# S5 tables formed unit by unit, with the chunk-state inputs taken from on-chip S tables inside the v projection slots

## The chip, the cores and the metric

One core of a Trainium2 chip runs the program. The metric is device time in microseconds (us) for one launch, as a median over runs. Engines are written as in the profile: PE is TensorE, PEld its weight loads, DVE VectorE, ACT ScalarE, POOL GpSimd, SP SyncE; SPq and ACTq are those engines' work of issuing DMAs. Matmul operands are split into a high and a low part (float32r), so a product of two matrices is three passes.

## The reference, cut to what matters

One layer works on 128 context tokens and 512 latent tokens (NT = 640). The part in question is the mixer: a chunked gating half (u, v) and a state-space half ("S5": 64 groups of 16 channels, one 64-dim complex state for each group and direction).

```
def ssm_discretize(lam_re, lam_im, log_dt, b_re, b_im):
    lam_bar = jnp.exp(lam * dt)
    b_bar = ((lam_bar - 1.0) / lam)[..., None] * b
    return lam_bar, b_bar
def ssm_scan(u, lam_bar, b_bar, h0, reverse):
    bu = jnp.einsum("gph,blgh->blgp", b_bar, u)
    _, h = lax.associative_scan(_scan_combine, (a, bu), axis=1, reverse=reverse)
def s5_mixer(...):
    y = (jnp.einsum("ghp,blgp->blgh", c_f, h_f) + jnp.einsum("ghp,blgp->blgh", c_b, h_b)).real
    y = gelu(y + d_skip * x);  y = y * sigmoid(y @ w_glu + b_glu)
def trunk_layer(...):
    u_a, v_a, u_b = jnp.split(h @ p["w_in"], [D_CHUNK, 2 * D_CHUNK], axis=-1)
    y_a = chunk_mlp_mixer(u_a, v_a, ...)      # per chunk of 128: u * (w_s @ rmsnorm(v) + b_s)
    y_b, hf, hb = s5_mixer(u_b, ...)
    mix = concatenate([rmsnorm(y_a), rmsnorm(y_b)]) @ p["w_out"]
```

## The kernel before

**Order of the work.** First the modulation and the first norm (h_chunk) run beside the projection of the S5 input (u_chunk); that order is set by a scheduler that works on the program as written. From line 433 on each instruction is kept in program order (all of these show line L445 in the profile), and a hand-written plan of slots sets it: `slot` (line 490) runs the phases sp, evac, act, dve, pe, end, and `at(t, phase, f)` puts a piece of work into slot t. Most slots hold one weight chunk: its load is issued two slots ahead (`raw_of`), its split into high (ACT, `hi_of`) and low part (DVE, `lo_of`, tile `wl`) one slot ahead, and its matmuls run in the slot. Chunks 0 to 15 are the v projection (slots 0 to 15; tile `ws`), 16 to 31 the u projection (slots 16 to 31), 32 to 47 half of the output projection (slots 33 to 48; tile `as`; slot 32 has no chunk), 48 to 55 the GLU. Elementwise work that belongs to no slot comes from a generator, `flow[0]`: `run_flow` takes operations from it until their noted cost reaches a number. In slots 0 to 15 it is `tables`, later `scan`.

**The S5 half by chunks of 8 positions.** The 640 positions give NJ = 81 columns of 8 (one is a zero). The S5 input goes from `u_chunk` to DRAM as `ud` (channel, position in the chunk, column), one store for each of 8 channel blocks, from the tile `us`. `tables` first multiplies the whole of b by the discretisation factor (24 DVE operations of 512 elements on `btab`), then builds, for each of 16 units of 4 groups (`unit`), the table St (chunk input to state, 6 DVE operations of 512 elements, transposed on PE as `sp`, evacuated as SS, stored to DRAM as `sd`), the table O (state to output, 6 operations of 576, stored as `od`) and the convolution kernel (`kp`, `ks`, stored as `kd`). After slot 16, `tables_done` closes that pool, loads the S5 input again as `U` (16 loads of 16 partitions, pieces of 81 elements) and the `sd` tables as `st_`; `s5_in` (line 784; four units in each of slots 17 to 20) multiplies them (tile `x1p`) into the scan's array X. From slot 21 `scan` runs on DVE in the flow. The slot after it ends is called e; from there `s5_rest` puts two units of `s5_out` (tile `yp`) into each slot, stores the result to DRAM (`yd`), loads it back by channel (`yc`), applies gelu, and after slot e + 10 the GLU follows. `ada_step` puts pieces of the modulation of the later layers (1 MB of weights, four matmuls `adaq`) into slots that the loop at line 1113 names.

**Tiles and names of the rows.** `us`, `vo` and other short-lived tiles share the tag t25 with two buffers; PSUM tiles named `sp`, `x1p`, `vtp`, `z`, `yp` share the tag px with two; `vc` is the v projection loaded back for the chunk mixer, transposed as `vtp`. `so` holds what `s5_out` loads (`od` by SP, `kd` by ACT). `aw` is a piece of modulation weights, `wr` a raw weight chunk.

Of the kernel before, what the change touches and what calls it, by code (L numbers as in the profile page):

```python
# [43 lines left out]
def build(nc, tc, a, out, tap=None):  # L44
# [254 lines left out]
    def u_chunk(kc0, nk):  # L299
        kb = slice(kc0, kc0 + nk)  # L300
        cpl = 8 // nk
        for cb in range(8):
# [12 lines left out]
            else:  # L315
# [6 lines left out]
                nc.gpsimd.dma_start(ud[cb * 128:(cb + 1) * 128], us)  # L322
# [8 lines left out]
    ctab, btab = [big[:, 2 * NT_ + t * 4096:2 * NT_ + (t + 1) * 4096].rearrange("p (i c) -> p i c", i=2) for t in range(2)]  # L331
# [251 lines left out]
    yad = dram("yad", [128, NT])  # L583
# [53 lines left out]
    SY.dma_start(ctab[:, 0, :], a["c1"])  # L637
# [8 lines left out]
    def ch(tab, i, d, g0, n):  # L646
        return mkap(tab, i * 2048 + (d * NG + g0) * GH, [[GH, 4], [0, n], [1, GH]])

    def tables():


        S.activation(btab[:, 1, :], btab[:, 1, :], AF.Copy, scale=nsgn)
        g3 = lambda t: t.rearrange("p (g h) -> p g h", h=GH)
        e_b = lambda t, s: t[:, s:s + 32].unsqueeze(2).broadcast_to([128, 32, GH])
        for s in range(0, 128, 32):
            b1, b2 = g3(btab[:, 0, s * GH:(s + 32) * GH]), g3(btab[:, 1, s * GH:(s + 32) * GH])
            u1 = g_.tile([128, 32, GH], F32, name="u1", tag="go", bufs=8)
            u2 = g_.tile([128, 32, GH], F32, name="u2", tag="go", bufs=8)
            V.tensor_tensor(u1, b2, e_b(ei, s), op=OP.mult)
            yield 0.7  # L660
            V.tensor_tensor(u2, b1, e_b(ei, s), op=OP.mult)
            yield 0.7
            V.tensor_tensor(b1, b1, e_b(er, s), op=OP.mult)
            yield 0.7
# [12 lines left out]
    kps = {}

    def unit(u):
        g0 = u * 4  # L680
        St = g_.tile([128, 2, 4, 8, GH], F32, name="St", tag="gs", bufs=4)
        for d in range(2):
            s0, st = (0, 1) if d == 0 else (7, -1)
            t2 = g_.tile([128, 4, 8, GH], F32, name="t3", tag="gt2", bufs=2)
# [16 lines left out]
        at(now[0] + 1, "pe", s_mm)
        if u == 0:
            V.tensor_scalar(ctab[:, 1, :], ctab[:, 1, :], -1.0, None, op0=OP.mult)
            yield 1.3
        O = [g_.tile([128, 4, 9, GH], F32, name="O", tag="go", bufs=8) for _ in range(2)]
# [43 lines left out]
        at(n + 1, "pe", k_copy)  # L749

# [12 lines left out]
    udv = ud.rearrange("(g c) t j -> t c g j", c=GH)  # L763
    ydv = yd.rearrange("(g c) t j -> t c g j", c=GH)
# [5 lines left out]
    Us, pbs, st_ = [], {}, {}  # L770
    X = None

    def u_load(half):
        U = pbs["uy"].tile([128, HG, NJ], F32, name="U", tag="uy", bufs=2)
        Us.append(U)
        for tq in range(8):
            SY.dma_start(U[(7 - tq) * GH:(8 - tq) * GH], udv[tq][:, half * HG:(half + 1) * HG, :])

    def st_load(u):
        if u < 16:  # L780
            st_[u] = pbs["pb"].tile([128, 2, 4, 128], F32, name="st_", tag="so", bufs=3)
            SY.dma_start(st_[u].rearrange("p d g c -> p (d g c)"), sd[u])

    def s5_in(u):

        for d in range(2):
            p = px("x1p")
            for g in range(4):
                gg = 4 * u + g
                T.matmul(p[:, g * NJ:(g + 1) * NJ], st_[u][:, d, g, :], Us[gg // HG][:, gg % HG, :], start=True, stop=True)  # L790
            pv = p[:, 0:4 * NJ].rearrange("p (g j) -> p g j", j=NJ)
# [933 lines left out]
```

## Time and profile before

| what | value |
|---|---|
| median of 3 runs | 2790.15 us (2788.37 to 2792.84) |
| the profiled execution's own time | 2791.73 us |
| its span | 2789.9 us |
| PE busy, of the span | 2625.2 us (94%) |
| DVE busy | 1942.8 us (70%) |
| ACT busy | 1102.2 us (40%) |
| mean granted TensorE clock | 0.962 of full speed |
| HBM traffic over the span | 190 GB/s |

The profile page has one execution. Busy shares are means over stages with different limits: the second half of the span (the MLP) has PE at 90% or more in nearly every slice, while the stage of this change, from some 235 us to 866 us, has slices with PE in the 60s and 70s of per cent and DVE anywhere from 10 to 90%. The rows below are from there. Slot numbers are put to times by counting the groups of `ws` and `as` matmuls.

### The profile page before, as it was taken

How to read it: one execution, taken by the hardware profiler on the slowest of the kernel's cores; microseconds unless marked ns; L12 is line 12 of the kernel's file. 1: busy time of each engine (PE TensorE's matmuls, PEld its weight loads, DVE VectorE, ACT ScalarE, POOL GpSimd, SP SyncE). 2: the span in 40 equal slices, each digit the busy share in tenths (PEclk: the TensorE clock that was granted, in tenths of full speed). 3: DMA queues.
4: the chain of work that ended last, by engine and by line, in shares of the span. 5: the costliest groups of instructions: out<-in, count | busy, mean ns of one | idle time of the engine just before them, and what ended most of it. 6: DMA issues, size and time to landing. Idle time of an engine off the chain costs nothing.

```text
span 2789.9 us, 42919 instructions
## 1 busy us (share of the span) xinstructions
PE 2625.2 (94%) x17217; PEld 2428.4 (87%) x17217; DVE 1942.8 (70%) x2839; ACT 1102.2 (40%) x1757; POOL 73.3 (3%) x89
## 2 busy tenths in 40 slices
PE   8998888999976997799999999999899999999997
PEld 5687778977765765799999999999899999999996
DVE  4567991689615455777777777777667777777786
ACT  4121321222213335655555555555433322333253
POOL 0000220000000000000000000000000000000000
PEclk9999998999967999899999999999999999999998
DMA  9846679554575686255555555556565355446453
GB/s 297 290 166 232 210 230 209 154 183 140 170 213 149 243 297 253 72 170 178 181 181 183 176 176 177 183 181 220 195 223 194 105 215 215 146 168 222 160 186 112
DMA packets 464231, 534.12 MB, mean 191 GB/s; under 512 B 34672, under 2 KB 377616, under 8 KB 456352
## 3 DMA queue, kind: packets, MB, share of 16 engines
q1 hardware_dynamic: 450288, 522.62, 57.9%
q10 hardware_dynamic: 13104, 6.10, 1.0%
q8 instruction: 136, 2.23, 0.3%
q0 software_dynamic: 640, 2.65, 0.3%
q14 instruction: 63, 0.52, 0.1%
HBM read 416.14 MB, written 115.16 MB: 190 GB/s over the span
## 4 chain that ended last, share of the span: by engine, by line
PE 78%; DVE 9%; DMA 7%; ACT 2%; issue 2%; SPq 1%; ACTq 0%; POOL 0%; DVEq 0%; POOLq 0%
PE X L1348 32%; PE Y L1348 16%; PE Z L1348 8%; PE ws L445 5%; PE ub L186 4%; PE as L445 4%; PE ob L1251 3%; PE ada L196 2%; DVE t L445 1%; DVE O L445 1%; DMA wr<-in_w_out_dram 1%; DVE St L445 1%; PE x1p L445 1%; DMA x2d<-wx 1%; PE adaq L445 1%
## 5 line engine op out<-in xcount | busy, mean ns | idle before, releaser
L1335 ACT ACTIVATE wh<-wx 128x1024 fp32r<-128x1024 f32 x223 | 235.9, 1058 | 310.5 <-PE X L1348 144.6
L1340 DVE TENSOR_TENSOR wl<-wx,wh 128x1024 fp32r<-128x1024 f32 x223 | 272.8, 1223 | 73.9 <-ACT wh L1335 71.9
L1348 PE MATMUL X<-B,wh 128*128 128x320 f32 x1376 | 306.1, 310 | 3.0 <-ACT wx L1335 3.0
L1348 PEld LDWEIGHTS X<-B,wh 128*128 128x128 f32 x1376 | 232.0, 189 | 3.2 <-ACT wx L1335 3.2
L1348 PE MATMUL X<-B,wl 128*128 128x320 f32 x688 | 213.2, 310 | 0.0
L1348 PE MATMUL Y<-B,wh 128*128 128x320 f32 x672 | 150.9, 313 | 4.7 <-ACT wh L1335 4.7
L1348 PE MATMUL X<-B,wx 128*128 128x320 f32 x1008 | 154.6, 309 | 0.0
L1348 PEld LDWEIGHTS X<-B,wx 128*128 128x128 f32 x1008 | 149.5, 188 | 0.0
L1423 DVE TENSOR_TENSOR wx<-wx 128x320 fp32r<-128x320 f32 x192 | 93.0, 485 | 77.9 <-ACT wx L1420 77.9
L1546 DVE TENSOR_TENSOR facc<-facc,X 128x640 f32<-128x640 f32 x116 | 95.1, 820 | 74.4 <-PE X L1348 73.7
L445 PE MATMUL ws<-hTh,wl 128*128 128x320 f32 x512 | 123.2, 323 | 21.0 <-DVE wl L445 21.0
L445 ACT ACTIVATE wh<-wr 128x1024 fp32r<-128x1024 f32 x56 | 59.4, 1060 | 192.5 <-DMA wr<-in_w_in_dram 58.1
L1348 PE MATMUL X<-B2n,wh 128*128 128x320 f32 x608 | 134.7, 309 | 0.0
L1348 PEld LDWEIGHTS X<-B,wl 128*128 128x128 f32 x688 | 130.1, 189 | 0.0
L445 PE MATMUL ws<-hTh,wh 128*128 128x320 f32 x512 | 125.0, 326 | 1.2 <-DVE us L321 1.2
L1335 ACT ACTIVATE wh<-wr 128x1024 fp32r<-128x1024 f32 x76 | 80.4, 1058 | 110.6 <-PE X L1348 51.5
L445 PE MATMUL ws<-hTl,wh 128*128 128x320 f32 x512 | 121.3, 319 | 0.0
L1335 ACT ACTIVATE wx<-wr 128x1024 fp32r<-128x1024 f32 x75 | 79.3, 1058 | 104.5 <-PE X L1348 49.0
L1335 ACT ACTIVATE wx<-wx 128x1024 fp32r<-128x1024 f32 x74 | 78.3, 1058 | 103.7 <-PE X L1348 48.4
L1348 PEld LDWEIGHTS Y<-B,wh 128*128 128x128 f32 x672 | 114.2, 191 | 4.9 <-ACT wh L1335 4.9
L1340 DVE TENSOR_TENSOR wx<-wr,wx 128x1024 fp32r<-128x1024 f32 x75 | 91.8, 1224 | 28.4 <-ACT wx L1335 27.6
L445 PEld LDWEIGHTS ws<-hTh,wl 128*128 128x128 f32 x512 | 90.0, 198 | 23.6 <-DVE wl L445 23.5
(411 smaller groups left out, 6651.8 us busy)
## 6 DMA issues: line engine op xcount, KB each, us to landing
wx<-in_w_ff_dram SPq DMA_DIRECT2D x169, 512.0 KB
x2d<-wx SPq DMA_DIRECT2D x224, 320.0 KB
wr<-in_w_ff_dram SPq DMA_DIRECT2D x87, 512.0 KB
aw<-in_w_ada_dram SPq DMA_DIRECT2D x80, 512.0 KB
was<-in_w_ada_dram SPq DMA_DIRECT2D x64, 512.0 KB
B2n<-x2d SPq DMA_DIRECT2D x24, 1280.0 KB
wr<-in_w_in_dram SPq DMA_DIRECT2D x48, 512.0 KB
wr<-in_w_out_dram SPq DMA_DIRECT2D x48, 512.0 KB
```

The lines of the kernel that those rows point to most:

```text
L186: T.matmul(p[:, :n], st[:, kk, c:c + 128], mv(k)[:, t0:t0 + n], start=(first and i == 0), stop=(last and i == 2))
L196: T.matmul(p[32 * j:32 * j + 32], sc[:, 2 * (k0 + i):2 * (k0 + i) + 32], w[:, i, :], start=k0 + i < 4, stop=k0 + i >= NK - 4)
L445: return lambda *p, **k: P(f(*p, **k))
L1251: T.matmul(p, st[:, k0 + kk, tsl], mv[:, kk, :], start=(k0 + kk == 0 and i == 0), stop=(k0 + kk == 7 and i == 2))
L1335: P(S.activation(hls[n][0], raw, AF.Copy))
L1340: P(V.tensor_sub(lo, raw, hi.bitcast(F32)))
L1348: P(T.matmul(p, st[:, j, c:c + 128], xv(j, x), start=first and j == 0 and i == 0, stop=j == nj - 1 and i == 2, skip_group_check=not first))
L1423: P(V.tensor_sub(hlt[i][:, 1], raw, hlt[i][:, 0].bitcast(F32)))
L1546: P(V.tensor_add(dst, dst, src))
```

## The change

In words, in the order of the program:

- `ud` becomes (partition = 16 x (7 - position in the chunk) + channel in the group, group, column). Each `us` is stored by 8 DMAs of 128 pieces of 81 elements (324 bytes) where one DMA of 128 pieces of 648 elements stood; for the first six channel blocks four of the eight are issued by ACT, the rest by POOL.
- b and c come as one array `bc`, 512 columns (256 KB) for each unit, three buffers, instead of four arrays of 1 MB. The powers of lambda and the factors er, ei are copied by ACT from `big` to `tabs`, and X takes the memory of `big` from then on.
- The 24 operations of 512 on all of b become 6 operations of 128 elements in each of 16 units. St has 2 buffers where it had 4, O 4 where it had 8.
- SS is not stored. `s5_in(u - 1)` runs in slots 2 to 16, in `s_mm(u)` ahead of the transposes of unit u, on SS and on `xin`, a load of 4 groups of `ud` (162 KB); ACT writes both directions into X, where ACT and DVE wrote one each.
- `sd`, `st_` and 16 loads of U go; U is loaded whole, in two DMAs of 128 partitions of 10 KB, after slot 16. The detour of ya through DRAM (`yad`) goes.
- `scan` starts in slot 17 (before: 21), `ada_step` is also called in slots 17 to 20, 36 and 40, and no longer from slot e to slot 48.

The core of the diff:

```diff
-                nc.gpsimd.dma_start(ud[cb * 128:(cb + 1) * 128], us)
+                for t in range(L):
+                    (nc.scalar if t % 2 and cb < 6 else nc.gpsimd).dma_start(
+                        bass.AP(tensor=ud.tensor, offset=ud.offset + ((7 - t) * GH * NG + cb * 8) * NJ,
+                                ap=[[NJ, 8], [NG * NJ, GH], [1, NJ]]), us[:, t, :])
...
+    tabs = g_.tile([128, 2 * NT_ + 256], F32, name="tabs")
+    bcs, xin = {}, {}
+    def bc_load(u):
+        if u < 16:
+            bcs[u] = g_.tile([128, 4, 2, 4, GH], F32, name="bc", tag="bc", bufs=3)
+            SY.dma_start(bcs[u].rearrange("p t d g h -> p (t d g h)"), a["bc"][:, u * 512:(u + 1) * 512])
+    bc_load(0)
     raw_of(0)
-    for i, nm in enumerate(("b1", "b2")):
-        SY.dma_start(btab[:, i, :], a[nm])
+    S.activation(tabs[:, 0:2 * NT_], big[:, 0:2 * NT_], AF.Copy)
+    S.activation(tabs[:, 2 * NT_:], big[:, 3712 + 9 * 128:3712 + 11 * 128], AF.Copy)
...
     raw_of(1)
+    bc_load(1)
+    bc_load(2)
     hi_of(0)
     lo_of(0)
+    X = a40([128, 2, NG, NJ + 1], F32, "X")
...
+    def u_unit(u):
+        xin[u] = g_.tile([128, 4, NJ], F32, name="xin", tag="xin", bufs=2)
+        SY.dma_start(xin[u], ud[:, 4 * u:4 * u + 4, :])
     def tables():
...
+        for u in range(16):
+            b1, b2, c1 = [bcs[u][:, t] for t in range(3)]
+            S.activation(b2, b2, AF.Copy, scale=nsgn)
+            S.activation(c1, c1, AF.Copy, scale=sgn)
+            e_b = lambda t: mkap(t, u * 4, [[NG, 2], [1, 4], [0, GH]])
...
+            V.tensor_tensor(u1, b2, e_b(ei), op=OP.mult)
+            V.tensor_tensor(u2, b1, e_b(ei), op=OP.mult)
+            yield 0.5
+            V.tensor_tensor(b1, b1, e_b(er), op=OP.mult)
+            V.tensor_tensor(b2, b2, e_b(er), op=OP.mult)
+            yield 0.5
             V.tensor_add(b1, b1, u1)
...
+    def s5_in(u):
+        SS, U = sss.pop(u), xin.pop(u)
+        for d in range(2):
+            p = px("x1p")
+            for g in range(4):
+                T.matmul(p[:, g * NJ:(g + 1) * NJ], SS[d][:, g * 128:(g + 1) * 128], U[:, g, :], start=True, stop=True)
+            S.activation(X[:, d, 4 * u:4 * u + 4, (1 - d):(1 - d) + NJ], p[:, 0:4 * NJ].rearrange("p (g j) -> p g j", j=NJ), AF.Copy)
...
         def s_mm():
-            SS = g_.tile([128, 2, 512], F32, name="SS", tag="gss", bufs=2)
+            if u:
+                s5_in(u - 1)
...
-            SY.dma_start(sd[u], SS.rearrange("p d c -> p (d c)"))
+        at(now[0] + 1, "sp", lambda: u_unit(u))
         at(now[0] + 1, "pe", s_mm)
...
+        at(n + 1, "pe", lambda: bc_load(u + 3))
...
-    for u in range(16):
-        at(17 + u // 4, "pe", lambda u=u: s5_in(u))
+    at(16, "pe", lambda: s5_in(15))
+    at(16, "end", lambda: tables_done())
...
-        if t == 21:
+        if t == 17:
             flow[0] = scan()
...
-        if scanned and e is None:
+        if scanned and e is None and t >= 38:
...
-            if 21 <= t < 32 or t > 34 and t % 4:
+            if 17 <= t < 32 or t > 34 and e is None:
                 ada_step(t)
-            slot(True, *((0, 0) if t < 21 else (2.0, 4.6) if t < 32 else (0.0, 2.0) if t == 33 else (2.0, 5.0)))
+            slot(True, *((0, 0) if t < 17 else (2.0, 4.6) if t < 32 else (0.0, 2.0) if t == 33 else (2.0, 5.0)))
```

**Where instructions move.** First ACT at the end of the S5 input projection, before: the splits of weight chunks (`wh`; L175 is `load_w`, L445 the slots), then the first table work.

```order
L256 ACTIVATE hTh_899<-tp,AS 128x128
L175 ACTIVATE wh<-wr 128x1024 x2
L445 ACTIVATE wh<-wr 128x1024 x2
L445 ACTIVATE big<-big,nsgn 128x2048
L445 ACTIVATE wh<-wr 128x1024
L445 ACTIVATE big<-big,sgn 128x2048
```

The same place on ACT in the change (L174 is `load_w`, L323 the stores of `us`, L447 the slots).

```order
L255 ACTIVATE hTh_898<-tp,AS 128x128
L174 ACTIVATE wh<-wr 128x1024
L323 DMA ud<-us 8x16x81 x8
L174 ACTIVATE wh<-wr 128x1024
L323 DMA ud<-us 8x16x81 x16
L447 ACTIVATE tabs<-big 128x2304
L447 ACTIVATE tabs<-big 128x256
L447 ACTIVATE wh<-wr 128x1024 x2
```

Twenty-four DMA issues and the two copies to `tabs` now stand ahead of the high parts of chunks 0 and 1; on POOL 40 issues stand where 8 stood.

Next PE in a v slot before, from the last matmuls of a chunk to the first of the next chunk.

```order
L445 MATMUL ws_3323<-hTh_224,wl 128x320
L445 MATMUL kp<-O,big 32x128 x8
L445 MATMUL sp<-ident,St 128x128 x8
L445 MATMUL kp<-O,big 32x128 x8
L445 MATMUL adaq<-aw,sc 32x512 x4
L445 MATMUL ws_3322<-hTh_899,wh 128x320
```

And PE in a v slot of the change.

```order
L447 MATMUL ws_2704<-hTh_223,wl 128x320
L447 MATMUL x1p<-xin,SS 128x81 x8
L447 MATMUL sp<-ident,St 128x128 x8
L447 MATMUL kp<-O,bc 32x128 x8
L447 MATMUL adaq<-aw,sc 32x512 x4
L447 MATMUL ws_2703<-hTh_898,wh 128x320
```

Each of 15 transposes of a unit in the v slots now has the 8 matmuls `x1p` of the unit before ahead of it; the 32 in each of slots 17 to 20 are gone, and unit 15's stand in slot 16.

Last SP where slot 16 passes into slot 17, before.

```order
L445 DMA wr<-in_w_in_dram 128x8x128
L445 DMA U<-ud 16x32x81 x8
L445 DMA st__4011<-sd 128x1024
L445 DMA st__4013<-sd 128x1024
L445 DMA st__4015<-sd 128x1024
L445 DMA U<-ud 16x32x81 x8
L445 DMA wst<-in_w_s_dram 128x128
L445 DMA bsb<-in_b_s_dram 128x128
L445 DMA vc<-vd 128x640
```

And the same place on SP in the change.

```order
L447 DMA wr<-in_w_in_dram 128x8x128
L447 DMA U<-ud 128x2592 x2
L447 DMA wst<-in_w_s_dram 128x128
L447 DMA bsb<-in_b_s_dram 128x128
L447 DMA vc<-vd 128x640
L447 DMA vd<-vo 128x640
```

Two large loads of U stand ahead of `vc` where 16 small ones and three of `st_` stood, and nothing in slots 17 to 20 loads a table. Further on, the first `yp` matmuls stand behind the 15th of the 16 `as` chunks before, and behind the 11th in the change: e is slot 47 before and slot 43 in the change.

## Rows read from the trace of the kernel before

**Rows 1.** Windows: length, busy (count) PE, PEld, DVE, ACT, POOL; clock, DMA, GB/s.

```profile
235.05:425.30 190.25, 166.40 (x1246) 148.48 (x1247) 174.16 (x240) 53.90 (x120) 42.02 (x58) 0.92 0.72 226
433.80:464.90 31.10, 22.10 (x119) 21.55 (x119) 5.51 (x20) 2.71 (x5) 0.00 (x0) 0.65 1.09 210
464.90:511.60 46.70, 46.55 (x363) 46.31 (x363) 11.06 (x19) 11.56 (x26) 0.00 (x0) 0.98 0.54 164
511.60:617.30 105.70, 99.67 (x700) 89.78 (x698) 90.75 (x216) 22.44 (x48) 9.42 (x5) 1.00 0.53 164
617.30:706.50 89.20, 83.47 (x377) 62.73 (x377) 83.61 (x195) 26.18 (x34) 3.19 (x2) 0.96 0.47 157
706.50:737.90 31.40, 31.40 (x146) 22.82 (x145) 29.93 (x73) 7.80 (x10) 0.00 (x0) 1.00 0.39 134
737.90:866.00 128.10, 88.40 (x529) 70.22 (x525) 27.93 (x51) 26.73 (x45) 0.00 (x0) 0.72 0.77 207
```

**Rows 2.** Timeline of PE in a v slot: start, us, operation, idle before.

```profile
353.66 0.67 PE L445 MATMUL kp<-O,big 128*32 128x128 f32 x16
...
354.26 1.09 PE L445 MATMUL sp<-ident,St 128*128 128x128 f32 x8
...
355.28 1.07 PE L445 MATMUL adaq<-aw,sc 128*32 128x512 f32 x8
...
358.97 0.56 PE L445 MATMUL ws<-hTh,wl 128*128 128x320 f32 x2 [1.82 <-DVE wl L445]
```

**Rows 3.** Groups by shape, 235 to 440 us: busy us, mean ns, idle before.

```profile
L445 DVE TENSOR_TENSOR St<-big 128x512 f32<-128x512 f32 x32 | 22.0, 688 | 0.0
...
L445 DVE TENSOR_TENSOR big<-big,u 128x512 f32<-128x512 f32 x8 | 5.5, 690 | 0.2
```

**Rows 4.** Waits, 235 to 440 us: total us, times, longest.

```profile
PE ws L445 <- DVE wl L445: 21.0, 9, 3.4
...
DVE big L445 <- DMA big<-in_c_dram: 4.4, 1, 4.4
```

**Rows 5.** Chain that ended last, 425 to 475 us: start, us, what.

```profile
433.93 7.79 DMA U<-ud
...
446.61 7.19 DMA U<-ud
...
453.87 6.51 DMA st__4180<-sd
```

**Rows 6.** Timeline of PE in slot 18: first and last of four units.

```profile
472.97 1.91 PE L445 MATMUL x1p<-U,st__4194 128*128 128x81 f32 x16
...
478.29 1.95 PE L445 MATMUL x1p<-U,st__4305 128*128 128x81 f32 x16
```

**Rows 7.** Groups of DVE by shape, 640 to 740 us.

```profile
L445 DVE TENSOR_TENSOR scq<-lam,X 64x128 f32<-64x128 f32 x80 | 31.3, 391 | 1.9
```

**Rows 8.** Chain that ended last, 735 to 870 us.

```profile
758.69 10.68 PE yp L445 x96
...
779.15 8.74 DMA yd<-U
...
795.88 8.54 DMA aw<-in_w_ada_dram
...
831.95 5.25 DMA yd<-U
```

**Rows 9.** Tile ud: POOL's issues (ns), who waited, time to landing.

```profile
L322 POOL DMA_DIRECT2D ud<-us x8: 539/542/712, 211.8 to 239.2; - x8
...
  POOL us L317: 17.4, 5
...
DMA to landing us min/median/max: 2.5/3.2/7.1
```

**Rows 10.** Timeline of ACT: four DMA issues.

```profile
747.87 2.44 ACTq L445 DMA_DIRECT2D so<-kd  x4
```

**Rows 11.** Window in which the yd stores move.

```profile
784.00:790.00 6.00, 3.44 (x14) 1.56 (x14) 0.00 (x0) 0.00 (x0) 0.00 (x0) 0.54 0.88 139
```

More of the change, by code (lines that the diff above doesn't have):

```diff
@@ L626, in v_evac @@
         at(now[0], "act", lambda: add_square(h, t))
+    tabs = g_.tile([128, 2 * NT_ + 256], F32, name="tabs")
[5 more added lines that the diff above has]
+    bc_load(0)
     raw_of(0)
-    for i, nm in enumerate(("b1", "b2")):
-        SY.dma_start(btab[:, i, :], a[nm])
+    S.activation(tabs[:, 0:2 * NT_], big[:, 0:2 * NT_], AF.Copy)
+    S.activation(tabs[:, 2 * NT_:], big[:, 3712 + 9 * 128:3712 + 11 * 128], AF.Copy)
+    Nre, Nim = [tabs[:, t * NT_:(t + 1) * NT_] for t in range(2)]
+    er, ei = [tabs[:, 2 * NT_ + t * 128:2 * NT_ + (t + 1) * 128] for t in range(2)]
     raw_of(1)
+    bc_load(1)
+    bc_load(2)
     hi_of(0)
     lo_of(0)
+    X = a40([128, 2, NG, NJ + 1], F32, "X")
     d16 = g_.tile([128, 16], F32, name="d16")
     id16 = g_.tile([128, GH], F32, name="id16")
-    SY.dma_start(ctab[:, 0, :], a["c1"])
     SY.dma_start(d16, a["ssm_d"])
@@ L644, in pw, with ch @@
         return mkap(tab, (d * NP + s0) * NG + g0, [[1, 4], [step * NG, n], [0, GH]])
-    def ch(tab, i, d, g0, n):
-        return mkap(tab, i * 2048 + (d * NG + g0) * GH, [[GH, 4], [0, n], [1, GH]])
-    def tables():
[L652 to L664, printed above, removed]
+    def ch(bc, t, d, n):
+        return mkap(bc, (2 * t + d) * 4 * GH, [[GH, 4], [0, n], [1, GH]])
@@ L697, in s_mm @@
                     T.transpose(p[:, g * 128:(g + 1) * 128], St[:, d, g].rearrange("p s c -> p (s c)"), ident)
-                S.activation(SS[:, d, :], p, AF.Copy)
-            SY.dma_start(sd[u], SS.rearrange("p d c -> p (d c)"))
+                S.activation(SS, p, AF.Copy)
+        at(now[0] + 1, "sp", lambda: u_unit(u))
         at(now[0] + 1, "pe", s_mm)
[L702 to L705, printed above, removed]
+        O = [g_.tile([128, 4, 9, GH], F32, name="O", tag="go", bufs=4) for _ in range(2)]
         for d in range(2):
@@ L730, in k_mm @@
                     c0 = (u % 2) * 256 + d * 128
-                    T.matmul(kp[32 * g:32 * g + 32, c0:c0 + 128], mkap(btab, (d * NG + g0 + g) * GH, [[1, 32]]),
+                    T.matmul(kp[32 * g:32 * g + 32, c0:c0 + 128], mkap(bc, (d * 4 + g) * GH, [[1, 32]]),
                              o.rearrange("p s c -> p (s c)"), start=True, stop=True)
@@ L769, in build @@
     JS = NJ + 1
-    Us, pbs, st_ = [], {}, {}
-    X = None
+    Us, pbs = [], {}
+    ydv = yd.rearrange("(g c) t j -> t c g j", c=GH)
     def u_load(half):
@@ L775, in u_load @@
         Us.append(U)
[L776 to L791, printed above, removed]
-            dst = X[:, d, 4 * u:4 * u + 4, (1 - d):(1 - d) + NJ]
-            if d:
-                V.tensor_copy(dst, pv)
-            else:
-                S.activation(dst, pv, AF.Copy)
-        st_load(u + 3)
+        SY.dma_start(U, ud[:, half * HG:(half + 1) * HG, :])
     def scan():
@@ L918, in u_evac @@
         y_ = zt
-        if 1 <= h < 6:
-            if h % 2:
+        if h < 6:
+            if h % 2 == 0:
                 ykeep.append(pbs["pb"].tile([128, 1536], F32, name="yk", tag="so", bufs=3))
-            y_ = ykeep[-1][:, (h + 1) % 2 * NT:(h + 1) % 2 * NT + NT]
+            y_ = ykeep[-1][:, h % 2 * NT:h % 2 * NT + NT]
         for n in range(2):
             V.tensor_mul(y_[:, n * 320:(n + 1) * 320], zt[:, n * 320:(n + 1) * 320], bank["u", h][n][:, :320])
-        if h == 0:
-            at(now[0] + 1, "sp", lambda: SY.dma_start(yad, zt))
-            at(now[0] + 3, "sp", ya_load)
         at(now[0] + 1, "act", lambda: add_square(h, y_))
@@ L972, in tables_done @@
     def tables_done():
-        nonlocal X
         pg.__exit__(None, None, None)
@@ L979, in tables_done @@
         pbs["pb"] = pbs["c"].__enter__()
-        X = a40([128, 2, NG, JS], F32, "X")
         u_load(0)
-        for u in range(3):
-            st_load(u)
         u_load(1)
-    at(16, "evac", tables_done)
-    def ya_load():
-        ya_[0] = pbs["pb"].tile([128, L * NJ], F32, name="ya", tag="ya", bufs=1)[:, 0:NT]
-        SY.dma_start(ya_[0], yad)
     def ya_tiles():
@@ L1684, in host_arrays @@
     cr, ci = [f(t)[0].transpose(3, 0, 1, 2).reshape(NS, 2048) for t in (ssm_c_re, ssm_c_im)]
-    r["b1"], r["b2"], r["c1"], r["c2"] = st(br, bi), st(bi, br), st(cr, ci), st(ci, cr)
+    bc = [t.reshape(128, 2, 16, 4, GH) for t in (st(br, bi), st(bi, br), st(cr, ci), st(ci, cr))]
+    r["bc"] = np.stack(bc, axis=1).transpose(0, 3, 1, 2, 4, 5).reshape(128, 8192)
     d = np.zeros((4, 32, 16), dtype=f(ssm_d).dtype)
```

35 lines of the change are left out of this document (15 added, 20 removed).

## The prediction

> **What bounds the kernel now.** I read the windows by stage first, cut where the slots change character [rows 1]. The reader is to see three limits. In the v stage (slots 0 to 15, 235.05 to 425.30) DVE is busy 174.16 of 190.25 us and PE 166.40. Who waits for whom there: PE waited 21.0 us in 9 stays for `wl`, the low part of a weight chunk, which DVE makes between table operations [rows 4]; a slot shows one such stay, 1.82 us, behind the table matmuls [rows 2]. So DVE sets the pace. In slot 17 (433.80 to 464.90) PE has 22.10 us of work, half of it at the lower of its two clock levels (mean granted clock 0.65, where 0.5 is 1.2 GHz and 1.0 is 2.4). The chain of waits names the cause: two loads of U of 7.79 and 7.19 us and one of `st_`, 6.51 us [rows 5]. Slots 18 to 20 are PE alone: 46.55 of 46.70 us, 15.6 a slot, DVE 11.06. Slots 21 to 31 take 105.70 / 11 = 9.61 us each with the scan on DVE. Then the tail: slots 47 to 57 take 128.10 us with PE busy 88.40, clock 0.72, and the chain there runs through yd, so, aw and yd again [rows 8], so DMA and its order set it, with DVE nearly free (27.93).
>
> **The change, part by part.** All times are against the profiled execution, 2791.73 us; the median of the runs shown is 2790.15, 1.6 lower.
>
> *Stores of the S5 input (before slot 0).* POOL issues a block in 0.54 us, it lands after 3.2 us (2.5 to 7.1), and POOL waited 17.4 us for buffers to come free [rows 9]. The change issues 4 on POOL (2.2 us) and 4 on ACT (2.44 us for four at the nearest row, [rows 10]), and 332 KB in small pieces need 2.4 us at the 139 GB/s that equally small stores reached at a DMA share of 0.88 [rows 11]. A block then takes some 6 us instead of 4. In return, POOL's order puts each store ahead of the next block's memset, where before the memset of block 5 stood ahead of the store of block 4, so two buffers overlap. I take 0, between -5 (the overlap wins) and +20 (below). By the Trainium skill (DMA: Bandwidth & Descriptors, Specifications) transfers under 512 B fall below line rate because they are read, changed and written back. The row of 139 GB/s, against 226 in the v stage's window, agrees in direction. By the row this place adds 0 to the sum; by the rule, up to the +20 of rival A.
>
> *v stage, PE.* `x1p` of a unit costs (478.29 - 472.97) / 3 = 1.77 us [rows 6]. Fifteen units come into the v slots: 26.6 us. PE has 190.25 - 166.40 = 23.9 us idle there, so 2.7 us do not fit.
>
> *v stage, DVE.* Out go 24 operations of 0.69 us [rows 3], 16.6, and a wait of 4.4 for c [rows 4]. In come 96 operations of 128 elements. The trace of before has none of this form. The lower end is the same elements at the price per element of the 512 form, 0.17 us each, 16.6 in all; the upper end the scan's 128-element operation, 0.391 [rows 7], 37.5. I take 0.27, 26 us, nearer the lower: bc is contiguous, the scan's operand is strided. DVE then has about 174 + 9 = 183 us of work: it still fits in 190. Both engines are now over 95% full and each waits for the other once a slot, so I add 4 us for bad meshing: v stage +7. Bounds: -5 if the wait for c and cold-clock stretches vanish without a price; +24 if all of the 21.0 us of waits stay beside PE's 2.7.
>
> *Other work of the v slots.* sd (512 KB) leaves each unit's DMA load, bc (256) and xin (162) come; ACT has busy 53.90 of 190, so the 15 pairs of X evacuations and 32 small scalings are covered there; without that cover each evacuation would cost PE its own length once a unit.
>
> *Slot 16.* One unit of `x1p`: +1.8.
>
> *Slot 17.* The waits of 21.5 us in the chain [rows 5] and the matmuls of four units leave. What is late next is `vc`: it is queued behind the two U loads (2.65 MB), which wait until slot 16's last PE work frees the pool. At 210 to 226 GB/s that is 12 us, against a chunk of 7 us and slot 16's end: I take 4 us of waiting, 0 to 13. Chunk 7.2, wait 4, `vtp` and `adaq` 2.2: 13.4 against 31.1, so -17.7.
>
> *Slots 18 to 20.* They become like slots 21 to 31: 3 x 9.61 = 28.8 against 46.70: -17.9. DVE, 11 us busy before, covers the scan that comes in.
>
> *Slots 32 to 42.* Two `adaq` steps more at 1.07 [rows 2]: +2.1. The GLU slots get two more as well: +2.1.
>
> *Tail.* e falls from slot 47 to 43. Before, slots 43 to 46 and the tail take 31.4 + 128.1 = 159.5 us. In the change slots 43 to 46 hold a chunk ((31.4 - 3 x 1.07) / 4 = 7.05) and two units of `yp` at 10.68 / 4 = 2.67 [rows 8]: 12.4 each, 50. Slots 47 to 50 hold units 8 to 15, which took 52.8 us before, from the first yd store at 779.15 to the second at 831.95 [rows 8]. Two chunks come in, mostly covered by PE's idle 40 us in this window; the aw pieces between leave, one of which alone held the chain for 8.54 us, and loads for the chunks come in their place: 51. The stretch from 832 to the GLU at 866, store, load, gelu, is unchanged: 34. Together 135 against 159.5: -24.5. Bounds 118 (aw's absence shortens all of it) and 150 (as chunks and so loads contend).
>
> **Sum.** +7 + 1.8 - 17.7 - 17.9 + 2.1 + 2.1 - 24.5 = -47.1. Against 2791.73 that is 2744.6; against the median 2743.1. I say 2744.
>
> **The rivals.**
> *A, the front holds the weights.* The splits of chunks 0 and 1 stand on ACT behind 24 issues, and in the built order SP's loads of bc and of chunk 0 wait for completion semaphores that stores of block 5 use. If the stores take the 7.1 us that the slowest landing took, five waits grow by about 4 us each: +20, so 2764. Against: the issues on ACT end two blocks before the stage does. The page named above speaks for this rival.
> *B, the load of U is only moved.* vc, the first scan step and the weight loads of slots 18 and 19 wait behind it as PE did before: the 13 us of the bound and 7 at the low clock, so +16: 2760. Against: pieces of 10 KB instead of 324 bytes.
> *C, a shorter tail.* 118 instead of 135: 2727. For it: DMA share 0.77 and the aw rows in the chain.
> *D, slower: PE and DVE take turns at St.* St has two buffers, and unit u's buffer comes free only after PE's transposes, which stand behind a whole chunk and `x1p`. If DVE reaches unit u + 2 before that, its six St operations (6 x 0.69 = 4.1 us) no longer lie beside PE work and a slot becomes 11.9 + 4.1. Over 14 slots that is +57, less the 4 of bad meshing, and the kernel ends at 2797. It decides from 3.4 us a slot on, where the 47 are eaten. Against: DVE's flow is about one slot behind PE's chunk, so in slots with one unit the transposes come some 10 us before the buffer is wanted.
> *E, small DVE operations at the upper price:* +11.5, of which the 7 spare us hide part; some 2752.
>
> **Chances.** Forecast 0.46 (its own range 2725 to 2762), A 0.14, B 0.09, C 0.15, D 0.09, E 0.07. The 80% range runs from C's lower side, 2712, to A and B together with a few us, 2774, which leaves out D and the ends. A measurement of this kernel can tell about 0.2% (5.6 us) from no change. Faster by more: all but D and the sum of A, B and E, 0.88; within 0.2%: 0.04; slower: 0.08.
>
> **What the profile will show.** v stage of about 197 us with PE over 95% busy, and PE's waits for `wl` mostly gone; if DVE waits for PE in front of St, D is at work. `x1p` at 1.8 us a unit inside v slots, and slots 18 to 31 at 9.6. A wait of PE for `vc` in slot 17 of a few us; above 13 it is B. First `yp` near 689 instead of 745 (706.5 + 7 - 24.7), and the GLU near 817 instead of 866. DVE operations of 128 elements near 0.27 us from start to start. Wrong it would be through the first matmul of slot 0 later than 245 (A), or a tail that grows as it takes in the five chunks.

## The result and the profile after

The changed kernel takes 2755.2 us (median; 2746.7 to 2757.4), the kernel before on the same chip 2789.5: ratio 0.987, 95% interval 0.985 to 0.989. The change makes it faster by 34 us where 47 were forecast.

The windows of the changed kernel, cut where [rows 1] was cut (same columns), show where:

```profile
250.40:439.21 188.81, 183.75 (x1488) 164.78 (x1488) 176.74 (x307) 74.75 (x178) 43.63 (x61) 0.99 0.69 206
449.18:460.75 11.57, 9.67 (x64) 7.72 (x63) 9.21 (x29) 1.54 (x3) 0.00 (x0) 0.94 0.75 234
460.75:491.01 30.26, 28.22 (x197) 26.07 (x193) 21.23 (x54) 7.89 (x16) 0.00 (x0) 0.97 0.44 138
491.01:598.90 107.89, 101.44 (x701) 91.31 (x697) 91.94 (x212) 22.58 (x48) 8.43 (x5) 0.98 0.53 168
598.90:688.19 89.29, 85.75 (x400) 61.48 (x401) 83.66 (x196) 26.44 (x34) 3.26 (x2) 1.00 0.53 180
688.19:824.16 135.97, 103.96 (x608) 85.90 (x605) 33.85 (x58) 33.14 (x53) 0.00 (x0) 0.83 0.64 180
```

They are the v stage, slot 17, slots 18 to 20, 21 to 31, 32 to 42, and the tail. In the v stage PE is now the fuller engine (183.75 of 188.81, clock 0.99); slot 17 has lost its long wait; the tail is 24 us shorter with more PE work in it. The account, with the first matmul of each stage in PE's timeline as its border (to some 0.4 us), us:

| stretch | before | after | moved | forecast |
|---|---|---|---|---|
| start to slot 1 | 249.87 | 260.56 | +10.7 | 0 |
| slots 1 to 15 | 175.4 | 178.7 | +3.2 | +7 |
| slot 16 | 8.5 | 10.0 | +1.5 | +1.8 |
| slot 17 | 31.1 | 11.6 | -19.5 | -17.7 |
| slots 18 to 20 | 46.7 | 30.3 | -16.4 | -17.9 |
| slots 21 to 31 | 105.7 | 107.9 | +2.2 | 0 |
| slots 32 to 42 | 89.2 | 89.3 | +0.1 | +2.1 |
| tail, to the first GLU matmul | 159.5 | 136.0 | -23.5 | -24.5 |
| GLU slots, to the first `ob` | 68.2 | 69.3 | +1.1 | +2.1 |
| out_b stage, to the first `Y` | 233.0 | 238.3 | +5.3 | 0 |
| rest | 1622.8 | 1623.5 | +0.7 | 0 |
| sum of the rows | 2789.9 | 2755.2 | -34.7 | -47.1 |

The front is cut at slot 1 and not at slot 0, because slot 0 of before began at 235.05 but then stood 3.4 us for `wl` behind the last add. By the prediction's own border, the start of slot 0, the front moved by +15.4 us (235.05 to 250.40) and the v stage by -1.4 (190.25 to 188.81, where +7 and "about 197" were forecast).

Two rows miss: the front, and the out_b stage, which the change does not touch. First the front. The view of the tile `ud` answers to [rows 9]; the line under "who waited" is DVE's:

```profile
L323 POOL DMA_DIRECT2D ud<-us x40: 597/597/776, 211.2 to 261.1; - x40
L323 ACTq DMA_DIRECT2D ud<-us x24: 587/587/699, 210.7 to 237.0; - x24
...
  DVE us L320: 16.4, 4
...
DMA to landing us min/median/max: 2.0/3.3/6.9
```

A store of 41 KB issued by POOL lands after 3.3 us in the median (ACT's landings are not in the trace), about as late as one of 332 KB did (3.2), and a block now needs eight. The adds into `us` waited 16.4 us for stores, 4.9 before by the same view. The timelines of DVE and ACT (start, us, operation, idle before) carry it on:

```profile
245.52 1.41 DVE L320 TENSOR_TENSOR us<-uacc,ub 128x128 f32<-128x128 f32 x3 [4.69 <-DMA ud<-us]
...
246.97 2.43 ACT L447 ACTIVATE tabs<-big 128x2304 f32<-128x2304 f32 x2 [28.75 <-DVE us L320]
249.30 1.99 ACT L447 ACTIVATE wh<-wr 128x1024 fp32r<-128x1024 f32 x2
```

The last adds start at 245.52 instead of 237.12. Behind them stands the copy of the N tables to `tabs`, and behind that on ACT the split of chunk 0; the first matmul of slot 0 came at 250.40. By the mark that the prediction set (245) this was rival A's result, though not, as the runs show, by A's mechanism in the main.

In the v slots (PE's timeline; it answers to [rows 2, 6]) a unit of `x1p` costs 1.85 us from start to start (1.74 or 1.85 in all of the units), and the transposes behind it 1.28 where they took 1.02:

```profile
326.56 2.01 PE L447 MATMUL x1p<-xin,SS 128*128 128x81 f32 x16
328.41 1.35 PE L447 MATMUL sp<-ident,St 128*128 128x128 f32 x8
329.69 1.06 PE L447 MATMUL adaq<-aw,sc 128*32 128x512 f32 x8
```

PE's waits for `wl`, 21.0 us in 9 stays before [rows 4], are 3.6 in 4 over the whole v stage:

```profile
PE ws L447 <- DVE wl L447: 3.6, 4, 1.3
```

Not all of the new work went into PE's idle time. From slot 1 on PE was idle 20.3 us before (175.43, less 155.16 busy) and 5.1 in the change: 15 of the 27 us of `x1p` went there. The clock gave back another part. Before, with PE 88% busy, a mean of 0.93 was granted, some 24 us of it at the lower level (0.5, which is 1.2 GHz); in the change, with PE 97% busy, it was 1.00 (2.4 GHz) throughout. So the same `ws` matmuls took 10 us less, before in the first line, the change in the second:

```profile
249.87:425.30 175.43, 121.20 (x718) 115.22 (x719) 0.00 (x0) 5.44 (x14) 0.93 0.73 228
260.56:439.21 178.65, 110.88 (x720) 105.75 (x720) 0.00 (x0) 5.34 (x14) 1.00 0.69 206
```

The new small DVE operations, by shape (they answer to [rows 3]):

```profile
L447 DVE TENSOR_TENSOR u<-bc,tabs 128x128 f32<-128x128 f32 x32 | 9.3, 330 | 2.8 <-ACT bc L447 2.7
L447 DVE TENSOR_TENSOR bc<-bc,tabs 128x128 f32<-128x128 f32 x32 | 7.9, 288 | 0.6
L447 DVE TENSOR_TENSOR bc<-bc,u 128x128 f32<-128x128 f32 x32 | 7.8, 285 | 0.0
```

25.0 us in all, 26 forecast. The Trainium skill (VectorE: DVE Perf Modes, The TRN2 errata) gives (N + 151) / 0.96 ns for an fp32 `tensor_tensor` addition, as it measured at N of 512 and 2048; at 128 that is an estimate of 291 ns. The row of additions and subtractions, 285, and one of multiplications, 288, are within 2% of it; the other multiplications, 330, take longer.

The chain in slots 17 and 19, and that of the tail, which answers to [rows 8]:

```profile
450.74 7.50 DMA vc<-vd
...
472.96 7.20 DMA vc<-vd
...
695.43 5.32 PE yp L447 x48
...
778.80 4.62 DMA so<-od
...
799.34 6.73 DMA yd<-U
```

The `aw` piece has left the chain of the tail; two units of `yp` take 5.32 (5.34 forecast), chunks of `as` lie between, and transfers of `so` and `yd` end it. First `yp` at 695 and GLU at 824, forecast 689 and 817: 6 and 7 us late, which is the front's 10.7 less some 4 that the rows behind it won over the forecast.

### The profile page after: what moved, and what is told of

It is laid out like the page before. It is cut to its first block, busy times and chain, and to the rows that moved or that the text cites. A ratio compares the mean times of both kernels' runs of the same rounds, so it can differ in the third digit from the quotient of the medians.

```text
span 2755.2 us, 43153 instructions
## 1 busy us (share of the span) xinstructions
PE 2607.8 (95%) x17217; PEld 2410.9 (88%) x17217; DVE 1939.6 (70%) x2894; ACT 1117.6 (41%) x1805; POOL 89.9 (3%) x121
## 4 chain that ended last, share of the span: by engine, by line
PE 82%; DMA 6%; DVE 6%; ACT 3%; issue 2%; SPq 1%; ACTq 1%; POOL 0%; DVEq 0%; POOLq 0%
PE X L1339 32%; PE Y L1339 16%; PE Z L1339 8%; PE ws L447 7%; PE ub L185 4%; PE as L447 3%; PE ob L1242 3%; PE ada L195 2%; DMA vc<-vd 1%; PE yp L447 1%; PE adaq L447 1%; DMA x2d<-wx 1%; PE adaq L195 1%; DMA wr<-in_w_out_dram 1%; PE x1p L447 1%
## 5 line engine op out<-in xcount | busy, mean ns | idle before, releaser
L1339 PEld LDWEIGHTS X<-B,wh 128*128 128x128 f32 x1376 | 232.0, 189 | 3.8 <-ACT wx L1326 3.8
L447 ACT ACTIVATE wh<-wr 128x1024 fp32r<-128x1024 f32 x56 | 59.2, 1059 | 193.7 <-DMA wr<-in_w_in_dram 72.2
L447 PE MATMUL ws<-hTh,wh 128*128 128x320 f32 x512 | 121.8, 320 | 12.1 <-ACT wh L447 12.1
L447 DVE TENSOR_TENSOR wl<-wr,wh 128x1024 fp32r<-128x1024 f32 x56 | 68.5, 1223 | 90.6 <-ACT wh L447 89.6
L447 PE MATMUL ws<-hTh,wl 128*128 128x320 f32 x512 | 119.1, 314 | 3.6 <-DVE wl L447 3.6
L447 PE MATMUL ws<-hTl,wh 128*128 128x320 f32 x512 | 118.2, 312 | 0.0
L447 PEld LDWEIGHTS ws<-hTh,wh 128*128 128x128 f32 x512 | 86.2, 192 | 30.5 <-issue 16.4
```

Source lines behind the costliest of these rows:

```text
L447: return lambda *p, **k: P(f(*p, **k))
L1339: P(T.matmul(p, st[:, j, c:c + 128], xv(j, x), start=first and j == 0 and i == 0, stop=j == nj - 1 and i == 2, skip_group_check=not first))
```

## The experiments

Twelve kernels were run, four to six times each. Times are compared by the ratio to the kernel before, which ran beside each of them. Slot borders of the experiments are counted from PE's timeline (48 matmuls a chunk).

A border comes from one profiled execution, and the front varies from one to the next. The changed kernel and five experiments that leave its front alone (scan21, u_late, x1p2, no_small, awr_pool) run the same instructions in the same order there, and slot 1 starts at 260.6, 262.1, 256.3, 260.6, 262.7 and 260.3. So a difference of 3 us in front of slot 1 tells nothing, and one of 12 does.

**f_flat**: one contiguous store a block.

```diff
-for t in range(L): (ACT or POOL).dma_start(ud piece t, us[:, t, :])
+nc.gpsimd.dma_start(<ud, flat, block cb>, us)
```

> The changed kernel, with each block of the S5 input stored as before the change: one contiguous transfer on POOL, none on ACT. The rearrangement is left out, so x1p and yp multiply numbers that stand in the wrong places, in unchanged shapes. Theory 1 (buffers): in the changed kernel the adds into us wait for buffers that eight small transfers give back late (last add at 245.52 us against 237.12 before), and the copies of the N tables and the split of chunk 0 wait behind the last add. Here slot 1 starts some 9 us earlier, near 251.5, and the kernel takes 2746. Theory 2 (issue): ACT's 24 issues and loads of SP that wait for their completions hold the weights; all that is gone too, also 2746. Theory 3 (the stores are not the cause, the table copies on ACT are): slot 1 stays within 2 us of 260.6, 2753 to 2755.

Ratio 0.979 (0.978 to 0.980), 2734.7 us, 11 below what theories 1 and 2 named. Slot 1 starts at 247.4 (260.6): 13.2 earlier, 4 more than they said, and the v slots give nothing back (slots 1 to 15: 178.7). Of the 22 us between the two spans 6 more are the out_b stage, 232.0 long (below). DVE's wait for buffers is nearly gone:

```profile
L322 POOL DMA_DIRECT2D ud<-us x8: 539/540/712, 211.6 to 233.8; - x8
...
  DVE us L320: 0.8, 1
DMA to landing us min/median/max: 2.5/2.8/5.8
```

So the stores set the front; theory 3 falls. The next three tell how.

**f_pool**: `nc.gpsimd.dma_start` for all 64 pieces.

> The changed kernel with all 64 small stores on POOL, none on ACT. Theory 1: POOL starts a store every 1.0 to 1.2 us, so a block takes 8 to 9 us where two queues took 6; the six blocks that wait for a buffer end 12 to 15 us later, slot 1 starts near 274 and the kernel takes 2768. Theory 2: ACT splits chunk 0 in time and SP's loads of bc and of chunk 0 no longer wait for the completion of stores: slot 1 near 252, 2746. Theory 3: no change, 2755.

0.989 (0.987 to 0.990). Slot 1 starts at 272.4, 11.8 later than in the changed kernel. POOL starts a store every 0.99 us in the mean, so a block takes 8, and DVE waits longer:

```profile
L323 POOL DMA_DIRECT2D ud<-us x64: 594/594/773, 210.1 to 272.4; - x64
...
  DVE us L320: 31.5, 6
DMA to landing us min/median/max: 2.0/2.2/6.3
```

The landings are earlier than in the changed kernel (2.2 in the median instead of 3.3), so here the time goes into the issues. With no issue on ACT the front is worse: theory 2, rival A as it was put, falls. Theory 1 had place and sign right (274 forecast); the kernel's time is less than its 2768, mostly since the out_b stage took 231.1.

**f_bufs**: eight places for `us`.

```diff
-us = main.tile([128, L, NJ], F32, name="us", tag="t25", bufs=2)
+us = big[:, 5120 + cb * 648:5120 + (cb + 1) * 648].rearrange("p (t j) -> p t j", t=L)
```

> The changed kernel with a place of its own for each of the eight us blocks (in the free half of big), stores as they are. Theory 1: no add waits for a store; the last add comes when PE is done with the last block, some 236 to 238 us, the table copies and the split follow, slot 1 starts near 253 and the kernel takes 2748. Theory 2: ACT still issues 24 stores and the loads of SP still wait for completions of block 5: slot 1 gains at most 3 us, 2752 to 2755. If instead the stores now crowd the later stage (x inputs of unit 0 read ud only after the last store), v slots 1 to 3 lose what slot 0 wins, 2755.

0.983 (0.982 to 0.984). The 24 issues are still on ACT; only the waits for buffers are gone. The table copies start at 235.31 instead of 246.97, slot 1 at 248.5. But slots 1 to 15 take 184.2, 5.0 of the 5.6 more in slot 2: `X` is laid over `big`, so its first evacuation waits for the stores, and in PE's timeline the transposes wait for it.

```profile
235.31 2.43 ACT L447 ACTIVATE tabs<-big 128x2304 f32<-128x2304 f32 x2 [8.79 <-DVE big L320]
...
269.55 0.77 ACT L447 ACTIVATE X<-x1p 128x324 f32<-128x324 f32 x2 [7.98 <-DMA ud<-big]
...
270.05 1.97 PE L447 MATMUL sp<-ident,St 128*128 128x128 f32 x8 [2.93 <-ACT X L447]
```

Theory 1 holds for the front. About half of the gain went to the new wait. The last sentence of the expectation had such a loss in v slots 1 to 3, but through the loads of `xin`, not through the place of `X`; slots 18 to 20 took 3.6 us more as well, which was not followed.

**f_order**: the split of chunk 0 ahead of the table copies.

```diff
-S.activation(tabs...) x2; raw_of(1); bc_load(1); bc_load(2); hi_of(0); lo_of(0)
+hi_of(0); raw_of(1); bc_load(1); bc_load(2); S.activation(tabs...) x2; lo_of(0)
```

> The changed kernel with the split of chunk 0 into its high part put ahead of the two table copies on ACT; stores as they are. Theory 1: the high part is ready by 240, the low part still waits behind the last add on DVE, 246.9 + 1.2: PE starts slot 0 near 248 instead of 250.4, the kernel takes 2752.5. Theory 2: the same or less. Theory 3: the copies were the cause, slot 0 starts near 241 and the kernel takes 2746.

0.986 (0.984 to 0.987); from the changed kernel's 0.987 it can't be told. The timelines of ACT and PE:

```profile
239.63 1.06 ACT L447 ACTIVATE wh<-wr 128x1024 fp32r<-128x1024 f32 x1 [21.06 <-DMA wr<-in_w_in_dram]
...
240.74 0.56 PE L447 MATMUL ws<-hTh,wh 128*128 128x320 f32 x2 [3.18 <-ACT wh L447]
...
247.72 0.90 PE L447 MATMUL ws<-hTh,wl 128*128 128x320 f32 x2 [6.12 <-DVE wl L447]
```

ACT waited for the load of chunk 0, so rival A's late loads are there; but they are covered, since PE, started at 240.74, waits next for the low part, which stands behind the last add on DVE as theory 1 had it. Slot 1 comes at 257.3, 3.3 earlier, which is no more than the front varies; so what the copies add behind the last add is not shown.

**f_dd**: contiguous stores, pieces moved between DRAM tensors in the v slots.

```diff
+nc.gpsimd.dma_start(ud0[cb * 128:(cb + 1) * 128], us)
+def ud_block(cb):   # ahead of slot 0, then at slots 0, 2, 4, ... 12
+    for t in range(L): G.dma_start(<ud piece t of block cb>, <ud0, block cb, column t>)
```

> The changed kernel, its result unchanged, with each us block stored by one contiguous transfer as before the change, and the small pieces moved afterwards, block by block, from one DRAM tensor to the other in v slots (64 transfers on POOL, two slots ahead of their use). Theory 1 (the small pieces cost only where us buffers wait for them): slot 1 starts near 247.5, as with the contiguous stores alone, and the v slots lose nothing: 2735 to 2740. Theory 2 (the pieces cost wherever they run, through the queues they share with weights): the v stage gives back 5 us or more, 2742 to 2750. The built order of the out_b stage is here the one that took 232 us with the contiguous stores, against 238 to 241 in three kernels with the order of the changed one; by order alone 232 again.

0.980 (0.978 to 0.982), 2738.5 us: with an unchanged result, faster than the kernel before and the changed one. Slot 1 at 246.0; slots 1 to 15 take 180.6, 2 more than in the changed kernel; out_b 234.2. The 64 small transfers take as long to issue and land no earlier:

```profile
L445 POOL DMA_DIRECT2D ud<-ud x64: 594/597/645, 233.6 to 387.1; - x64
...
DMA to landing us min/median/max: 2.2/3.6/6.5
```

(The landings of the eight large stores are among these; the 64 alone have a median of 3.7.) So the small transfers cost some 13 us where buffers wait for them and about 2 where nothing does.

**scan21**: the scan from slot 21, and the `ada_step` pieces placed as before.

```diff
-if t == 17: flow[0] = scan()
+if t == 21: flow[0] = scan()
-if 17 <= t < 32 or t > 34 and e is None:
+if 21 <= t < 32 or t > 34 and t % 4:
```

> The changed kernel with the scan begun in slot 21 and the ada steps placed as before the change; everything else of the change stays. Theory 1 (the forecast: the earlier scan carries the tail): e falls back to slot 47, the tail from slot 43 on takes 159 us again (+23.5); slots 18 to 20 without scan take 8.5 us each instead of 10.1 (-5), two ada steps leave slots 32 to 42 (-2); the out_b stage, whose built order is near that of before here, loses 5. Together 2755 + 11.5 = 2766. Theory 2 (the tail is set by its transfers, whenever the scan ends): the tail stays at 136 and the kernel takes 2743.

0.991 (0.989 to 0.993), 11 us over the changed kernel, by ratios. From the first `as` to the first `ob` 308.4 us (changed kernel 287.4, before 310.9); slots 18 to 20 take 23.9, 6.4 less. First `yp` comes 122.0 us after the first `as` (changed kernel 89.2, before 121.8), so e is back at slot 47. The chain between 715 and 850 has `aw` back in it:

```profile
755.47 6.53 DMA so<-kd
762.08 8.54 DMA yd<-U
...
810.03 12.02 DMA aw<-in_w_ada_dram
```

Theory 1 holds, with a sum right within its interval: without the earlier scan the kernel loses 21 us from the first `as` to the first `ob`, gains 6 in slots 18 to 20 and 4 in the out_b stage. The run puts two things back at once, the scan's start and the `ada_step` pieces; that e goes back to 47 is the scan's doing, but how much of the 21 us the pieces alone would cost was not tried.

**u_late**: `u_load` at slots 33 and 34.

> The changed kernel with the two loads of U in slots 33 and 34 instead of the end of slot 16. Theory 1 (rival B in small: vc and the first scan steps queue behind 2.65 MB): slot 17 falls from 11.57 to some 9.6 us, slots 18 and 19 by about 1 each; 2751. Theory 2: vc is late in every second slot up to 31 whatever stands ahead of it, so nothing moves: 2755. If U now holds up the loads of the output tables from slot 35 on, the first yp comes later and the kernel takes 2758.

0.987 (0.985 to 0.989): no change. Slot 17 falls to 8.8, under the other experiments' 9.9 to 12.7. Slots 18 to 20 take 32.6 instead of 30.3, where the other kernels with the early scan have 29.2 to 34.0, and from first `as` to first `yp` it is 93.4 against 89.2 (88.0 to 90.5 in those others). PE's waits for `vc` between 440 and 520, this kernel's first, then the changed one's:

```profile
PE vtp L447 <- DMA vc<-vd: 3.4, 2, 2.0
```

```profile
PE vtp L447 <- DMA vc<-vd: 5.3, 3, 2.0
```

2 us of wait go, and 4 come back ahead of the first `yp`, as the last sentence of the expectation allowed. Rival B's wait is real and small.

**x1p2**: each `x1p` matmul twice.

> The changed kernel with the matmuls of x1p done twice over, to the same result: 15 units more in the v slots, one in slot 16, at 1.74 us. Theory 1 (PE has become the bound of the v stage): slot 1 to slot 16 grows by 21 to 26 us from 178.65, slot 16 by 1.7, the kernel takes 2779 to 2783. Theory 2 (DVE still sets the pace, PE waits for wl or St in each slot): less than 10 us, under 2766.

0.994 (0.992 to 0.996): 20 us over the changed kernel, 2777.2, 2 under what theory 1 named. Slots 1 to 15 take 200.5, +21.8, slot 16 +1.8. The v stage of this kernel and of the changed one, from slot 1 (cut within 0.3 us of the borders):

```profile
260.60:461.30 200.70, 199.29 (x1677) 182.82 (x1674) 166.32 (x289) 71.35 (x173) 29.52 (x52) 1.00 0.61 184
```

```profile
260.56:439.21 178.65, 173.59 (x1436) 155.89 (x1432) 166.73 (x290) 71.63 (x172) 39.33 (x53) 1.00 0.69 206
```

PE's busy time grew by 25.7 and the stretch by 22.1: the new work took 3.7 of the 5.1 idle us and pushed the rest out. Theory 1.

**no_small**: the 96 operations left out.

> The changed kernel without the 96 DVE operations of 128 elements in the v stage; so the input table stays unscaled and the S5 numbers differ, in unchanged shapes. They are 25.0 us of busy DVE there. Theory 1 (PE is the bound of the v stage now): slot 1 to slot 16 stays within 5 us of 178.6, the most that PE's waits for wl give back. Theory 2 (DVE shares the bound, rival E): 15 to 25 us less. The built order of the out_b stage differs from all others, so the verdict is by the slots and not by the kernel's time, 2740 to 2756.

0.983 (0.982 to 0.985). Slots 1 to 15 take 173.1, 5.5 less (the window is cut 0.3 us late):

```profile
262.70:436.10 173.40, 171.98 (x1438) 156.30 (x1435) 146.02 (x197) 72.14 (x176) 36.57 (x55) 1.00 0.71 215
```

DVE lost 20.7 us of busy time; the stretch lost 5, 3.6 of them PE's idle time (5.1 before, 1.4 here). Just past the bound that theory 1 set, far from theory 2's.

**The out_b stage.** In the built programs SP issues its loads `awr` and `wr` in one of two orders there, alike but for the last two `awr`. In the timeline of SP before (start, us, loads):

```profile
1078.52 0.37 SPq L1168 DMA_DIRECT2D awr<-in_w_ada_dram  x1
1081.12 0.37 SPq L172 DMA_DIRECT2D wr<-in_w_out_dram  x1
1082.93 0.37 SPq L1168 DMA_DIRECT2D awr<-in_w_ada_dram  x1
1084.03 10.87 SPq L172 DMA_DIRECT2D wr<-in_w_out_dram  x3
```

and in the changed kernel:

```profile
1039.46 3.90 SPq L1159 DMA_DIRECT2D awr<-in_w_ada_dram  x2
1043.45 12.46 SPq L171 DMA_DIRECT2D wr<-in_w_out_dram  x4
```

One weight load has moved behind the second `awr`. Seven kernels with the first order (before, f_flat, f_pool, f_dd, scan21, no_small, dd_order) took 231.1 to 234.6 us for the stage, five with the second (changed, f_bufs, f_order, u_late, x1p2) 237.6 to 240.6.

**awr_pool**: `nc.gpsimd.dma_start` for the loads of `awr`.

> The changed kernel with the 24 loads of awr in the out_b stage issued by POOL instead of SP; all else as in the changed kernel. So far seven runs fall in two groups by SP's built order in that stage: where a load of wr stands ahead of the second of two late awr loads, as before the change, the stage takes 231 to 235 us; where it stands behind them, as in the changed kernel, 238 to 241. Theory 1 (a wr load waits in SP's line behind an awr load that waits for PE): off that line the stage takes 233 or less, the kernel 2750. Theory 2 (the stage is set by how many bytes its transfers move, 56 MB, or by the order on PE): it stays at 238 or more, 2755 to 2760.

0.994 (0.993 to 0.995), stage 253.6: both theories missed. In POOL's line 13 of the 24 loads stood for the landing of an earlier one:

```profile
POOL awr L1159 <- DMA awr<-in_w_ada_dram: 93.0, 13, 12.1
...
PE adaq L195 <- DMA awr<-in_w_ada_dram: 17.0, 7, 10.2
```

A new wait of `awr` covers what the run was to show. (Slots 21 to 32 also took 6.7 us more than in the changed kernel, which was not followed.) That the order in which the scheduler builds the stage goes with its length is shown by twelve kernels; that the one load is the cause is not.

**dd_order**: f_dd with f_order's edit.

> A candidate: contiguous stores with the pieces moved afterwards (the kernel of 0.980), and the split of chunk 0 put ahead of the table copies on ACT. With the small pieces gone from the front, the low part follows the last add at 238 us either way: slot 1 gains at most 2 us. SP's order in the out_b stage has wr ahead of the second awr: 231 to 235. 2735 to 2739.

0.982 (0.980 to 0.983), 2742.1 us, above the range named and no better than f_dd: slot 1 starts 2.4 earlier than in f_dd, which is no more than the front varies, and slots 1 to 15 take 185.6. Slot 4 alone is 17.6 us long (11.6 in f_dd), where ACT waits for weights and PE for `X`; what SP's line holds there was not followed further. From ACT's timeline:

```profile
286.72 1.06 ACT L445 ACTIVATE wh<-wr 128x1024 fp32r<-128x1024 f32 x1 [9.16 <-DMA wr<-in_w_in_dram]
```

**dd_order_awr**: both edits on f_dd.

> The candidate of the run before with the loads of awr on POOL as well. If the wait of wr behind awr in SP's line is what the out_b stage loses, it had little left to lose here, since its order was the good one: 228 to 233, the kernel 2732 to 2738. If POOL's line is worse for awr (its loads come later, adaq on PE waits), the stage takes 238 or more and the kernel 2742.

0.992 (0.990 to 0.993), stage 259.2: POOL's line again, worse than the miss that the expectation allowed.

## Why the prediction was right, and where it was off

The time is within the range and 11 us over the 2744 forecast; the sign is as forecast. Step by step:

- *Stores of the S5 input, 0 with bounds -5 and +20.* The step that failed; the front lost 10.7 us. The prediction had the numbers (a block in 6 us instead of 4, two buffers, a `us` that DVE must wait for) and let an order of memset and store win them back. Its term for POOL was too small: it took four issues at 0.54 us, 2.2 us; in the changed kernel POOL's 40 stores start 1.3 us apart in the mean. f_flat prices the small stores at 13.2 us in front of slot 1, f_bufs shows that the wait is for buffers (12.1 back with ACT's issues left in place), f_pool that issues on ACT are not it. Behind the last add the copies to `tabs` and the split of chunk 0 stand on ACT, a path that the prediction did not count; f_order moved the copies and won 3.3 us, no more than the front varies, so their part is not shown. Rival A had the size nearly right (+20 for the whole) and the reason, in the main, wrong. A piece of its kind is in the chain: POOL sat idle 2.0 us, by the profile until a load of `bc` landed, ahead of the store at 241.83 whose landing the last add waited for.
- *The rule of 512 B,* which the prediction weighed, is not needed for this: in f_dd pieces of the same size land no earlier and cost 2 us, and in f_pool they land after 2.2 us in the median. No run stores a block as eight transfers of long pieces, so number and size are not fully separated. The Trainium skill (DMA: Bandwidth & Descriptors, Anatomy of one DMA) gives for a DMA that GpSimd issues a fixed cost of 2.0 us plus bytes at 436 GB/s, by its figures an estimate of 2.1 us for 41 KB and 2.8 for 332 KB. The landings of POOL's stores agree about: 2.0 at the least and 2.2 in the median in f_pool for 41 KB, 2.5 and 2.8 in f_flat for 332 KB. The 3.3 of the changed kernel lies above.
- *v stage, +7.* +3.2 from slot 1 on, -1.4 by the prediction's own border. That `x1p` fills PE's idle time is right, and x1p2 shows that PE is the bound now. The size came out by terms that the prediction did not weigh: of 27 us of `x1p` the idle time took 15 and not all, the full clock gave 10 back (the prediction had "cold-clock stretches" in its lower bound only), and the transposes took 2.5 more. So the closeness is in part luck. The 4 us for bad meshing were about the right size: PE is left with 5.1 us of idle time, and no_small puts what is left of DVE's hold at 5. Rival D (turns at `St`) did not occur: no row of the waits from 235 to 440 us has DVE at `St` waiting for PE.
- *Small DVE operations, 0.27 each.* 0.26 on average; E falls.
- *Slot 16, slot 17, slots 18 to 20.* Forecast +1.8, -17.7, -17.9; measured +1.5, -19.5, -16.4. The wait for `vc` is there as named, 1.9 us where 4 were taken.
- *Tail, -24.5.* -23.5, and not by luck: its three terms, 50, 51 and 34, came out at 49.4 (slots 43 to 46), 51.4 (to the second group of `yd` stores at 789.0) and 35.2. e fell from 47 to 43, and scan21 gives that back when the scan starts late, together with the old places of the `ada_step` pieces. C (118 us) did not come.
- *Slots 32 to 42 and GLU, +2.1 each.* +0.1 and +1.1. In slots 32 to 42 PE's busy time did grow by 2.3 us (83.47 to 85.75), into its idle time.
- *Not in the sum:* slots 21 to 31, +2.2; out_b, +5.3, which goes with an order that the scheduler built anew. No reading of the diff shows it, a comparison of the built orders does; what in the order costs the time stays open.

## What to carry to other kernels

Where a store feeds a small ring of buffers, count transfers times issue interval and landing against the producer's turn; one big store and a later rearrangement in an idle queue kept some 13 us here. Moving matmuls into slots with idle PE is nearly free up to that idle time and at full price beyond it (x1p2: 25.7 us of work, 22.1 us longer); look too at the clock that is granted before and after, which gave back 10 us here. Compare built orders also in stages that the change does not touch: a stage built in another order took 5 us more here. And profile more than one kernel with the same front before a difference of 3 us is read from it.

## What the runs showed of the hardware

ACT issues small stores in a row one every 0.63 us, at 0.59 each: eight took 5.15 us. The second line below is 16 issues in one row, but in the trace it has semaphore waits of 0.9 to 3.1 us between groups of four, so it is no measure of the interval:

```profile
210.69 5.15 ACTq L323 DMA_DIRECT2D ud<-us  x8
220.83 16.77 ACTq L323 DMA_DIRECT2D ud<-us  x16
```

POOL's issues take 0.59 too, but start 0.6 to 2.8 us apart, 0.99 in the mean in f_pool; for 20.1 us in 28 places the profile names nothing that POOL waited for, so the cause is open.

Eight transposes behind `x1p` took 1.28 us from start to start in 12 of 15 units, 0.96 in unit 0 of the same kernel, which has no `x1p` ahead, and 1.28 again in x1p2 with twice the `x1p`; why was not tried.
